# A seven-product feed-forward: four plain pairs first instead of two, the activations' sums on VectorE, and later products added in PSUM to copies that ScalarE writes there

## The chip, the cores and the metric

The kernel runs on one core of one Trainium2 chip. The metric is the device time of one execution in microseconds, and the time of a kernel is the median of its runs. The names of the engines in the rows are PE for TensorE, DVE for VectorE, ACT for ScalarE, POOL for GpSimd and SP for SyncE.

## The reference

Two layers of a hybrid backbone run over 640 tokens, 128 context tokens and 512 latent ones, with 1024 features. Each layer is a modulated norm, an input projection, four parallel mixers, a gated merge with an output projection, and then a second modulated norm with a SwiGLU feed-forward, which is what the change touches:

```python
def _swiglu(h, w1, w2):
    a = jnp.dot(h, w1)                     # (tokens, 1024) x (1024, 2 * 2816)
    gt, up = jnp.split(a, 2, axis=-1)
    return jnp.dot(jax.nn.silu(gt) * up, w2)

sh1, sc1, gt1, sh2, sc2, gt2 = _adaln(cvec, w_mod[l], b_mod[l])
x = x + gt1 * _merge(...)
x = x + gt2 * _swiglu(_modulate(_rmsnorm(x, norm2_g[l]), sh2, sc2), w_ffn_in[l], w_ffn_out[l])
```

All of it is float32. The shift, scale and gate rows come from an adaLN product of a condition vector with w_mod, twelve chunks of 512 columns a layer.

## The kernel before

Every float32 product is made of three fp32r matmuls: each operand is split into a rounded part (hi, a cast on ScalarE) and a remainder (lo, a subtraction on VectorE), and hi x hi, hi x lo and lo x hi are summed in PSUM. `split` (L450 to L453, rows L451 and L452) does this for activations and feed-forward halves, and `wload` (rows L402 and L403) for whole weight blocks. The matmuls of most of the kernel are issued by `mm3` (L414 to L416).

The activations of a layer lie transposed in `hT`: eight blocks of 128 features, two parts, 640 tokens. The feed-forward has 22 pairs of 128 gate columns and 128 up columns. They are worked in four groups of 6, 6, 6 and 4 pairs (`FF_SPLIT`), and after each group its 128-row pieces are multiplied with the down projection (`residual_tm`, or `norm_tm` after the last).

The first `FF_PLAIN` = 2 pairs of a layer are plain: gate and up are each computed for the tokens in two column groups of 256 and 384, with 8 x 3 matmuls for each, and the results go through `silu` (L1900) and `cb` (L1903). The other 20 pairs are seven-product pairs, a form of Winograd's variant of Strassen's multiplication. The two halves of the features and the two halves of the tokens (320 each) give A11, A12, A21 and A22. The feature halves of the gate's and the up's columns give B11, B21 (gate) and B12, B22 (up). The four results are the gate and the up of either half of the tokens, and they need seven products of half blocks instead of eight, each of 4 x 3 matmuls with 320 columns.

`ff_sums` (L1728) makes the sums of activations S1, S2, S3 and S4, one of four feature blocks at a time: two additions hi + lo of 128x640 (L1735), four sums and differences of 128x320 (L1740 to L1743) and three splits. S1 takes the place of A21 in `hT`, split once the last plain pair has read it (the splits at the end of the plain pairs in `layer`). `ff_sums` is a generator: `layer` runs two of its four steps after each of the two plain pairs, and all steps are done after the second.

`ff_load` (L1759) loads four half blocks of weights for a pair into a ring of six half buffers and makes the four differences t1 to t4 on GpSimd (L1770 to L1773). It then splits the seven operands in the order in which the products use them, through the rings `hi_ring` and `lo_ring` of five.

`ff_pair` (L1790) issues the seven products and what combines them. Three accumulators come from the ring `acc` of three banks and one from `bO`. VectorE adds the products out of PSUM into SBUF tiles (L1817, L1821, L1824, L1831, L1837), ScalarE copies the first product (L1814) and applies SiLU (L1828, L1832), and `out` (L1807) multiplies (L1809) and splits.

Between all this runs background work: `adaln_all` accumulates the adaLN chunks of this layer and of the next (L473, L475, L477 and L479, on ScalarE, GpSimd and VectorE), transposes the sums (`adaln_cols`, L481) and reduces them. `tick` takes a step of it at a rate of 0.2 for each step of the projections.

The program is written in one order. A planner that simulates the engines (`schedule_with_timeline_sim`) then lays down the order on each engine, by readiness and by the priorities that the code gives (`WPRI` for weights, `EPRI` for evictions). That order is fixed when the kernel runs.

Of the kernel before, what the change touches and what calls it, by code (L numbers as in the profile page):

```python
# [13 lines left out]
AF = mybir.ActivationFunctionType  # L14
ALU = mybir.AluOpType
AX = mybir.AxisListType

P = 128
# [59 lines left out]

FF_SPLIT = (6, 6, 6, 4)

FF_PLAIN = 2
HALF = 320

WPRI = 20000
EPRI = 500
# [139 lines left out]
def trunk(ctx: ExitStack, tc: tile.TileContext, a: dict, depth: int):  # L225
    nc = tc.nc
    V, S, G, T, SY = nc.vector, nc.scalar, nc.gpsimd, nc.tensor, nc.sync
# [116 lines left out]
    acc = ring("acc", 3, [P, 512], F32, pq)  # L344
    bS = ring("S", 2, [P, 512], F32, pq)
    bT = ring("T", 2, [P, 512], F32, pq)
    bO = ring("O", 1, [P, 512], F32, pq)
    bigs = Slots("big", 1, 5120)

    def r32(t, n=1280):  # L350
        return t[:, :n]
# [23 lines left out]
    hT = cp.tile([P, KT, 2, NTOK], F32R, name="hT")  # L375
# [31 lines left out]
    def run(gen):  # L407
        for _ in gen:
            tick()
# [40 lines left out]
    def split(hi, lo, src):  # L450
        i = S.copy(hi, src)  # L451
        V.tensor_tensor(lo, src, hi.bitcast(F32), ALU.subtract)  # L452
        return i  # L453
# [27 lines left out]
    def adaln_cols(dst, accs):  # L481

        for v in range(2):
            ps = (bT if v else bS)()
            for j in range(4):
                T.transpose(ps[:, j * P:(j + 1) * P], accs[v][:, P * j:P * j + P], ident)
            V.tensor_reduce(dst(v), ps.rearrange("p (j n) -> p j n", j=4), AX.X, ALU.add)
# [1240 lines left out]
    def ff_sums(held, s1):  # L1728

        sop = [[r32(held[2 * i + x]).rearrange("p (k w n) -> p k w n", k=2, w=2) for x in range(2)] for i in range(3)]  # L1730
        for k in range(4):
            x = [p640().rearrange("p (h n) -> p h n", h=2) for _ in range(2)]
            for i, c0 in enumerate((0, HALF)):
                hi, lo = [hT[:, k:k + 5:4, w, c0:c0 + HALF].bitcast(F32) for w in range(2)]
                (V if i and k % 2 == 0 else G).tensor_tensor(x[i], hi, lo, ALU.add)  # L1735
            (a11, a12), (a21, a22) = [(t[:, 0, :], t[:, 1, :]) for t in x]
            z = p640()
            s2, s3 = z[:, :HALF], z[:, HALF:]
            t1 = s1[:, HALF * k:HALF * k + HALF]
            V.tensor_tensor(t1, a21, a22, ALU.add)  # L1740
            V.tensor_tensor(s2, t1, a11, ALU.subtract)
            V.tensor_tensor(s3, a11, a21, ALU.subtract)
            V.tensor_tensor(a12, a12, s2, ALU.subtract)  # L1743
            for i, t in enumerate((s2, s3, a12)):
                o = sop[i][k // 2][:, k % 2]
                split(o[:, 0], o[:, 1], t)
            yield
# [11 lines left out]
    def ff_load(l, j, spare, ts):  # L1759

        parts = ff_halves(spare)
        with tc.high_priority(offset=WPRI):
            def half(tile, h):
                off, x = PLAN[("fi", tile)]
                t = parts()
                SY.dma_start(t, a["wflat"][l, off:off + P * x].rearrange("(p x) -> p x", p=P)[:, 512 * h:512 * h + 512])
                return t
            b11, b12, b22, b21 = half(2 * j, 0), half(2 * j + 1, 0), half(2 * j + 1, 1), half(2 * j, 1)
            t1, t2, t3, t4 = [t[:, :512] for t in ts]
            G.tensor_tensor(t1, b12, b11, ALU.subtract)  # L1770
            G.tensor_tensor(t2, b22, t1, ALU.subtract)
            G.tensor_tensor(t3, b22, b12, ALU.subtract)
            G.tensor_tensor(t4, b21, t2, ALU.subtract)  # L1773
        for x in (b11, t2, t3, t1, b21, t4, b22):
            with tc.high_priority(offset=WPRI):
                hi, lo = hi_ring()[:, :512], lo_ring()[:, :512]
                split(hi, lo, x)
            yield hi, lo
# [10 lines left out]

    def ff_pair(ops, b, at):  # L1790

        pa, pb, pc, pd = [t[:, :HALF] for t in (acc(), acc(), acc(), bO())]
        x, y, z = f640(), f640(), f640()
        h1, h2 = slice(0, HALF), slice(HALF, NTOK)
        u2, u3 = z[:, h1], z[:, h2]

        def prod(ps, name, first):
            w = next(b)

            more = dict(skip_group_check=not first)  # L1800
            for k in range(4):
                f = lambda part: w[part][:, k * P:(k + 1) * P]
                T.matmul(ps, f(0), ops[name](k, 0), start=first and k == 0, stop=False, **more)  # L1803
                T.matmul(ps, f(0), ops[name](k, 1), start=False, stop=False, **more)  # L1804
                T.matmul(ps, f(1), ops[name](k, 0), start=False, stop=k == 3, **more)  # L1805

        def out(sl):  # L1807
            with tc.high_priority(offset=EPRI):
                V.tensor_tensor(x[:, sl], x[:, sl], y[:, sl], ALU.mult)  # L1809
                split(at[:, 0, sl], at[:, 1, sl], x[:, sl])  # L1810

        prod(pa, "A11", True)
        with tc.high_priority(offset=EPRI):
            S.copy(u3, pa)  # L1814
        prod(pb, "S2", True)
        with tc.high_priority(offset=EPRI):
            V.tensor_tensor(u2, pb, u3, ALU.add)  # L1817
        yield
        prod(pc, "S3", True)
        with tc.high_priority(offset=EPRI):  # L1820
            V.tensor_tensor(u3, pc, u2, ALU.add)  # L1821
        prod(pd, "S1", True)
        with tc.high_priority(offset=EPRI):
            V.tensor_tensor(y[:, h2], pd, u3, ALU.add)  # L1824
        yield
        prod(pa, "A12", False)
        with tc.high_priority(offset=EPRI):
            S.activation(x[:, h1], pa, AF.Silu)  # L1828
        prod(pc, "A22", False)
        with tc.high_priority(offset=EPRI):  # L1830
            V.tensor_tensor(x[:, h2], pc, u2, ALU.add)  # L1831
            S.activation(x[:, h2], x[:, h2], AF.Silu)  # L1832
        yield
        out(h2)
        prod(pd, "S4", False)
        with tc.high_priority(offset=EPRI):
            V.tensor_tensor(y[:, h1], pd, u2, ALU.add)  # L1837
        out(h1)
        yield

    def layer(l, *start):
        d = {"of": {}, "m": [], "mg": []}
# [31 lines left out]
        sums = ff_sums(held, s1)  # L1874
        for g, cnt in enumerate(FF_SPLIT):
# [4 lines left out]
            for jx in range(cnt):  # L1880
                j = j0 + jx
# [9 lines left out]
                sl = pl.take(F32R)  # L1891
                at = r32(sl).rearrange("p (w n) -> p w n", w=2)
# [14 lines left out]
                for groups in (LATE, EARLY) if j == 0 else (GROUPS,):  # L1907
# [2 lines left out]
                        hook()  # L1910
                        hook = None
                    run(fm(wu, KT, hmov, cb, groups))
                next(sums, None)
                next(sums, None)
                if j == FF_PLAIN - 1:
                    for _ in sums:
                        pass
                    for k in range(4):
                        split(hT[:, k, 0, HALF:], hT[:, k, 1, HALF:], s1[:, HALF * k:HALF * k + HALF])
                    qs.give(s1)  # L1920
            if g == 0:
                gts = gate_rows(l, 1)
            if g == 3:
# [119 lines left out]
```

## Time and profile before

| | us |
|---|---|
| median of 3 runs | 2818.46 |
| lowest and highest run | 2810.98, 2820.67 |
| the profiled execution | 2822.84 |
| its span, first to last instruction | 2821.0 |
| TensorE busy | 2701.9 |
| VectorE busy | 2175.1 |
| ScalarE busy | 1440.7 |
| GpSimd busy | 782.8 |
| mean granted clock of TensorE | 0.982 |

Busy time of TensorE is the time in which at least one matmul is in flight; successive matmuls overlap, so the rate at which they are done is read from their start times. A granted clock of 1.00 is 2.4 GHz and 0.5 is 1.2 GHz; a number between them is a mean over both. The feed-forward of the first layer lies at about 950 to 1430 us, that of the second at about 2360 to 2800 us.

### The profile page before, as it was taken

What the parts mean: (1) busy time and instruction counts of PE and PEld (TensorE: products, weight loads), DVE (VectorE), ACT (ScalarE), POOL (GpSimd) and SP (SyncE); (2) the same over time, 40 slices, a digit from 0 to 9 for tenths busy, and PEclk for the clock granted to TensorE, in tenths of its full rate; (3) what the DMA queues carried; (4) which work ended last, traced back from release to release, by engine and by line L of the source; (5) the groups of instructions that cost most, each with busy time, mean ns of one, the idle gap of its engine ahead of it and who ended that gap; (6) DMA issues with size and microseconds to landing.
All of it is one profiled execution on the core that took longest, in us unless ns stands there. A gap on an engine that the chain in (4) does not pass through costs nothing.

```text
span 2821.0 us, 51942 instructions
## 1 busy us (share of the span) xinstructions
PE 2701.9 (96%) x19466; PEld 2642.6 (94%) x19466; DVE 2175.1 (77%) x4800; ACT 1440.7 (51%) x3314; POOL 782.8 (28%) x678
## 2 busy tenths in 40 slices
PE   8999999999999879999999999999999999999998
PEld 4998999999999768999899999999999999899998
DVE  7767768888973897978677867778888847876967
ACT  6864446665653443434358654456666534433423
POOL 2001212120132564453430101212111334353433
PEclk9999999999999889999999999999999999999999
DMA  7224322121233233232232323222121331322222
GB/s 282 88 85 123 96 78 83 53 73 59 68 121 128 87 115 120 79 109 90 68 108 92 107 85 120 89 72 76 48 81 57 124 123 61 92 74 90 80 82 79
DMA packets 124734, 264.30 MB, mean 94 GB/s; under 512 B 14321, under 2 KB 40273, under 8 KB 124481
## 3 DMA queue, kind: packets, MB, share of 16 engines
q1 hardware_dynamic: 124480, 260.97, 29.1%
q8 instruction: 153, 2.51, 0.4%
q14 instruction: 101, 0.82, 0.1%
HBM read 252.73 MB, written 7.95 MB: 92 GB/s over the span
## 4 chain that ended last, share of the span: by engine, by line
PE 74%; DVE 14%; ACT 5%; issue 3%; DMA 2%; POOL 1%; SPq 0%; DVEq 0%; POOLq 0%; ACTq 0%
PE acc L414 16%; PE acc L415 16%; PE acc L416 16%; PE acc L1803 3%; PE acc L1805 3%; PE acc L1804 3%; PE O L1224 2%; PE T L1214 2%; DVE msum L479 2%; DVE wlo L403 2%; DVE wlo L452 1%; DMA raw<-wflat 1%; PE O L1803 1%; PE O L1804 1%; PE O L1805 1%
## 5 line engine op out<-in xcount | busy, mean ns | idle before, releaser
L414 PE MATMUL acc<-hT,whi 128*128 128x256 f32 (+1 forms) x2112 | 667.0, 318 | 28.1 <-DVE hT L669 10.5
L415 PE MATMUL acc<-hT,whi 128*128 128x256 f32 (+1 forms) x2112 | 666.1, 316 | 6.0 <-DVE hT L670 4.5
L416 PE MATMUL acc<-hT,wlo 128*128 128x256 f32 (+1 forms) x2112 | 662.7, 314 | 1.0 <-DVE wlo L403 1.0
L402 ACT CAST whi<-raw 128x512 fp32r<-128x512 f32 (+1 forms) x472 | 289.4, 619 | 436.6 <-PE acc L415 172.8
L403 DVE TENSOR_TENSOR wlo<-raw,whi 128x512 fp32r<-128x512 f32 (+1 forms) x472 | 358.2, 764 | 145.9 <-ACT whi L402 135.1
L414 PEld LDWEIGHTS acc<-hT,whi 128*128 128x128 f32 x2112 | 404.2, 192 | 35.1 <-DVE hT L669 11.4
L415 PEld LDWEIGHTS acc<-hT,whi 128*128 128x128 f32 x2112 | 405.3, 192 | 9.5 <-DVE hT L670 5.7
L416 PEld LDWEIGHTS acc<-hT,wlo 128*128 128x128 f32 x2112 | 404.6, 192 | 2.1 <-DVE wlo L403 1.1
L475 POOL TENSOR_TENSOR msum<-msum,mtmp 128x512 f32<-128x512 f32 x140 | 210.9, 1507 | 267.8 <-ACT msum L473 153.9
L1604 POOL TENSOR_TENSOR m<-m,f 128x256 f32<-128x256 f32 x96 | 100.1, 1046 | 523.5 <-DVE f L1602 346.8
L1632 POOL TENSOR_TENSOR big<-big,t 128x256 f32<-128x256 f32 x150 | 122.2, 823 | 304.0 <-DVE t L1631 296.5
L1631 DVE TENSOR_TENSOR t<-acc,P 128x256 f32<-128x256 f32 x200 | 83.1, 420 | 122.6 <-PE acc L416 94.9
L729 ACT CAST pth<-T 128x512 fp32r<-128x512 f32 (+1 forms) x232 | 118.1, 521 | 114.7 <-PE T L1214 56.2
L730 DVE TENSOR_TENSOR ptl<-T,pth 128x512 fp32r<-128x512 f32 (+1 forms) x232 | 137.4, 601 | 41.7 <-ACT pth L729 39.7
L451 ACT CAST whi<-of 128x512 fp32r<-128x512 f32 x160 | 98.8, 619 | 134.7 <-PE acc L1804 54.8
L1803 PE MATMUL acc<-hT,whi 128*128 128x320 f32 x480 | 152.1, 317 | 13.5 <-DVE f L1821 8.8
L414 PE MATMUL acc<-whi,m 128*128 128x256 f32 x560 | 158.2, 284 | 5.2 <-DVE t L1631 5.1
L414 PE MATMUL acc<-big,whi 128*128 128x256 f32 (+1 forms) x512 | 159.0, 311 | 0.9 <-ACT f L1596 0.9
L415 PE MATMUL acc<-big,whi 128*128 128x256 f32 (+1 forms) x512 | 159.0, 311 | 0.0
L416 PE MATMUL acc<-big,wlo 128*128 128x256 f32 (+1 forms) x512 | 158.7, 311 | 0.0
L415 PE MATMUL acc<-wlo,m 128*128 128x256 f32 x560 | 157.8, 282 | 0.2 <-DVE wlo L403 0.2
L416 PE MATMUL acc<-whi,m 128*128 128x256 f32 x560 | 157.2, 281 | 0.0
(465 smaller groups left out, 8189.5 us busy)
## 6 DMA issues: line engine op xcount, KB each, us to landing
raw<-wflat SPq DMA_DIRECT2D x228, 512.0 KB
wm<-w_mod SPq DMA_DIRECT2D x160, 256.0 KB
raw<-wflat SPq DMA_DIRECT2D x131, 256.0 KB
q<-wflat SPq DMA_DIRECT2D x53, 256.0 KB
kv<-nbias SPq DMA_DIRECT2D x16, 576.0 KB
kv<-mdr SPq DMA_DIRECT2D x16, 320.0 KB
big<-x_sample SPq DMA_DIRECT2D x8, 512.0 KB
P<-gt_d SPq DMA_DIRECT2D x32, 128.0 KB
```

Of the source, the lines that this page charges most:

```text
L402: S.copy(hi[:, :n], raw[:, s0:s0 + n])
L403: V.tensor_tensor(lo[:, :n], raw[:, s0:s0 + n], hi[:, :n].bitcast(F32), ALU.subtract)
L414: T.matmul(ps, lhs(k, 0), rhs(k, 0), start=(k == 0), stop=False)
L415: T.matmul(ps, lhs(k, 0), rhs(k, 1), start=False, stop=False)
L416: T.matmul(ps, lhs(k, 1), rhs(k, 0), start=False, stop=(k == kn - 1))
L475: G.tensor_tensor(accs[v][:, :512], accs[v][:, :512], tmp, ALU.add)
L729: S.copy(hi[:, :n], ps[:, :n])
L730: V.tensor_tensor(lo[:, :n], ps[:, :n], hi[:, :n].bitcast(F32), ALU.subtract)
L1632: (V if n == 3 else G).tensor_tensor(xs[tt][:, 256 * n:256 * n + 256], xs[tt][:, 256 * n:256 * n + 256], t[:, :256], ALU.add)
L1803: T.matmul(ps, f(0), ops[name](k, 0), start=first and k == 0, stop=False, **more)
L1804: T.matmul(ps, f(0), ops[name](k, 1), start=False, stop=False, **more)
L1805: T.matmul(ps, f(1), ops[name](k, 0), start=False, stop=k == 3, **more)
```

## The change

Four pairs of a layer are plain instead of two, and one step of `ff_sums` follows each of them. All eight hi + lo additions of `ff_sums` are on VectorE; before, six of the eight were on GpSimd. In a seven-product pair the products are issued in another order (A11, S3, S2, A12, S1, A22, S4), and two of VectorE's additions are replaced: ScalarE copies the first bank into a bank of the ring S, the product of S2 is added onto that copy in PSUM, ScalarE copies the sum into the second bank of S and into SBUF, and the product of S1 is added onto that. The last half's multiplication reads its bank directly. The weights are loaded and subtracted in the order that this needs. The banks of the ring S are written once by a matmul with `start=True` after the plain pairs (`ff_prime`), so that later matmuls without it add to what stands there, and `adaln_cols` no longer uses that ring.

```diff
-FF_PLAIN = 2
+FF_PLAIN = 4
...
     def adaln_cols(dst, accs):
         for v in range(2):
-            ps = (bT if v else bS)()
+            ps = bT()
...
             for i, c0 in enumerate((0, HALF)):
                 hi, lo = [hT[:, k:k + 5:4, w, c0:c0 + HALF].bitcast(F32) for w in range(2)]
-                (V if i and k % 2 == 0 else G).tensor_tensor(x[i], hi, lo, ALU.add)
+                V.tensor_tensor(x[i], hi, lo, ALU.add)
...
-            b11, b12, b22, b21 = half(2 * j, 0), half(2 * j + 1, 0), half(2 * j + 1, 1), half(2 * j, 1)
+            b12, b22, b11, b21 = half(2 * j + 1, 0), half(2 * j + 1, 1), half(2 * j, 0), half(2 * j, 1)
             t1, t2, t3, t4 = [t[:, :512] for t in ts]
+            G.tensor_tensor(t3, b22, b12, ALU.subtract)
             G.tensor_tensor(t1, b12, b11, ALU.subtract)
             G.tensor_tensor(t2, b22, t1, ALU.subtract)
-            G.tensor_tensor(t3, b22, b12, ALU.subtract)
             G.tensor_tensor(t4, b21, t2, ALU.subtract)
-        for x in (b11, t2, t3, t1, b21, t4, b22):
+        for x in (b11, t3, t2, b21, t1, t4, b22):
...
-        pa, pb, pc, pd = [t[:, :HALF] for t in (acc(), acc(), acc(), bO())]
+        pa, pb, pc, pd = [t[:, :HALF] for t in (acc(), bS(), acc(), bS())]
...
-        u2, u3 = z[:, h1], z[:, h2]
+        u2, p7 = z[:, h1], z[:, h2]
...
-        def out(sl):
-            with tc.high_priority(offset=EPRI):
-                V.tensor_tensor(x[:, sl], x[:, sl], y[:, sl], ALU.mult)
-                split(at[:, 0, sl], at[:, 1, sl], x[:, sl])
+        early = lambda: tc.high_priority(offset=EPRI)
         prod(pa, "A11", True)
-        with tc.high_priority(offset=EPRI):
-            S.copy(u3, pa)
-        prod(pb, "S2", True)
-        with tc.high_priority(offset=EPRI):
-            V.tensor_tensor(u2, pb, u3, ALU.add)
+        with early():
+            S.copy(pb, pa)
+        prod(pc, "S3", True)
+        with early():
+            S.copy(p7, pc)
         yield
-        prod(pc, "S3", True)
-        with tc.high_priority(offset=EPRI):
-            V.tensor_tensor(u3, pc, u2, ALU.add)
-        prod(pd, "S1", True)
-        with tc.high_priority(offset=EPRI):
-            V.tensor_tensor(y[:, h2], pd, u3, ALU.add)
+        prod(pb, "S2", False)
+        with early():
+            S.copy(pd, pb)
+            S.copy(u2, pb)
+        prod(pa, "A12", False)
+        with early():
+            S.activation(x[:, h1], pa, AF.Silu)
         yield
-        prod(pa, "A12", False)
-        with tc.high_priority(offset=EPRI):
-            S.activation(x[:, h1], pa, AF.Silu)
+        prod(pd, "S1", False)
+        with early():
+            V.tensor_tensor(y[:, h2], pd, p7, ALU.add)
         prod(pc, "A22", False)
-        with tc.high_priority(offset=EPRI):
+        with early():
             V.tensor_tensor(x[:, h2], pc, u2, ALU.add)
             S.activation(x[:, h2], x[:, h2], AF.Silu)
         yield
-        out(h2)
+        with early():
+            V.tensor_tensor(x[:, h2], x[:, h2], y[:, h2], ALU.mult)
+            split(at[:, 0, h2], at[:, 1, h2], x[:, h2])
         prod(pd, "S4", False)
-        with tc.high_priority(offset=EPRI):
-            V.tensor_tensor(y[:, h1], pd, u2, ALU.add)
-        out(h1)
+        with early():
+            V.tensor_tensor(x[:, h1], pd, x[:, h1], ALU.mult)
+            split(at[:, 0, h1], at[:, 1, h1], x[:, h1])
         yield
+
+    def ff_prime():
+
+        for _ in range(2):
+            T.matmul(bS()[:, :HALF], hT[:, 0, 0, :P], hT[:, 0, 0, :HALF], start=True, stop=True)
...
-                next(sums, None)
-                next(sums, None)
+                next(sums)
                 if j == FF_PLAIN - 1:
-                    for _ in sums:
-                        pass
                     for k in range(4):
                         split(hT[:, k, 0, HALF:], hT[:, k, 1, HALF:], s1[:, HALF * k:HALF * k + HALF])
                     qs.give(s1)
+                    ff_prime()
```

## Rows read from the trace of the kernel before

**Rows 1.** The page, part 1: busy us of each engine, share, instructions.

```profile
PE 2701.9 (96%) x19466; PEld 2642.6 (94%) x19466; DVE 2175.1 (77%) x4800; ACT 1440.7 (51%) x3314; POOL 782.8 (28%) x678
```

**Rows 2.** Windows: stretch, its us, busy us of PE, PEld, DVE, ACT, POOL; clock, DMA.

```profile
955.00:998.00 43.00, 34.86 (x208) 33.59 (x208) 41.73 (x55) 19.98 (x42) 30.77 (x20) 0.85 0.30 98
998.00:1083.00 85.00, 64.76 (x362) 59.88 (x360) 84.19 (x112) 39.82 (x77) 50.17 (x33) 0.86 0.39 122
1132.20:1205.80 73.60, 73.60 (x507) 73.60 (x507) 67.05 (x95) 35.44 (x70) 29.27 (x20) 1.00 0.27 81
1365.90:1419.90 54.00, 48.27 (x300) 46.63 (x299) 41.42 (x61) 23.10 (x46) 18.01 (x12) 0.94 0.24 76
2395.80:2453.00 57.20, 52.05 (x338) 50.14 (x337) 52.17 (x83) 28.48 (x59) 19.80 (x13) 0.97 0.32 94
2730.00:2783.20 53.20, 48.90 (x330) 47.80 (x329) 44.91 (x65) 24.55 (x49) 16.61 (x12) 1.00 0.29 95
```

**Rows 3.** Timeline of TensorE: start us, us, operation (single matmuls).

```profile
991.17 0.28 PE L414 MATMUL acc<-hT,whi 128*128 128x256 f32 x1
...
993.91 0.33 PE L414 MATMUL acc<-hT,whi 128*128 128x384 f32 x1
...
998.07 0.31 PE L1803 MATMUL acc<-hT,whi 128*128 128x320 f32 x1
...
1132.26 0.31 PE L1803 MATMUL acc<-hT,whi 128*128 128x320 f32 x1
...
1205.58 0.31 PE L1805 MATMUL O<-kv,wlo 128*128 128x320 f32 x1
```

**Rows 4.** Waits of TensorE, 955 to 1083: us, times, longest us.

```profile
PE acc L1803 <- ACT hT L451: 6.2, 1, 6.2
```

**Rows 5.** Groups of VectorE, 998 to 1083: busy us, mean ns, idle before.

```profile
L479 DVE SCALAR_TENSOR_TENSOR msum<-wm,csil,msum 128x512 f32<-128x512 f32 x19 | 20.7, 1088 | 0.0
L452 DVE TENSOR_TENSOR wlo<-of,whi 128x512 fp32r<-128x512 f32 x16 | 16.6, 1041 | 0.3 <-ACT whi L451 0.3
...
L1809 DVE TENSOR_TENSOR f<-f,f 128x320 f32<-128x320 f32 x6 | 5.1, 844 | 0.0
L452 DVE TENSOR_TENSOR m<-f,m 128x320 fp32r<-128x320 f32 (+2 forms) x6 | 4.6, 774 | 0.0
L452 DVE TENSOR_TENSOR wlo<-q,whi 128x512 fp32r<-128x512 f32 x4 | 4.3, 1084 | 0.0
...
L1821 DVE TENSOR_TENSOR f<-acc,f 128x320 f32<-128x320 f32 x4 | 1.9, 477 | 0.0
```

**Rows 6.** Timeline of VectorE, single instructions.

```profile
959.42 0.81 DVE L1735 TENSOR_TENSOR P<-hT 128x640 f32<-128x640 f32 x1
...
1023.18 0.68 DVE L452 TENSOR_TENSOR wlo<-of,whi 128x512 fp32r<-128x512 f32 x1
1023.78 0.74 DVE L479 SCALAR_TENSOR_TENSOR msum<-wm,csil,msum 128x512 f32<-128x512 f32 x1
```

**Rows 7.** Groups of GpSimd, 955 to 1083.

```profile
L1735 POOL TENSOR_TENSOR P<-hT 128x640 f32<-128x640 f32 x6 | 11.5, 1936 | 1.4 <-DVE kv L452 1.4
...
L1771 POOL TENSOR_TENSOR of<-raw,of 128x512 f32<-128x512 f32 x3 | 4.8, 1605 | 0.0
```

**Rows 8.** Two lines of VectorE: duration ns min/median/max over the span.

```profile
L1821 DVE TENSOR_TENSOR f<-acc,f x40: 475/478/492, 1029.8 to 2776.3; 128x320 f32<-128x320 f32 x40
...
L1809 DVE TENSOR_TENSOR f<-f,f x80: 477/486/1606, 1038.0 to 2784.2; 128x320 f32<-128x320 f32 x80
```

**Rows 9.** Waits of TensorE in the last group of the first layer.

```profile
PE acc L1803 <- DVE f L1821: 4.3, 2, 2.3
```

**Rows 10.** Timeline of TensorE and ScalarE at a pair's end, second group.

```profile
1157.04 0.31 PE L1803 MATMUL acc<-hT,whi 128*128 128x320 f32 x1
...
1160.05 0.46 ACT L451 CAST m<-f 128x320 fp32r<-128x320 f32 x1 [2.22 <-DVE f L1809]
...
1160.94 0.42 ACT L1814 COPY f<-acc 128x320 f32<-128x320 f32 x1
```

## The prediction

> **What bounds the kernel now.** I read the page's engine shares first: TensorE is busy for 2701.9 of 2821.0 us [rows 1]. A gain therefore lies where TensorE stands still or runs at the lower clock, and the second view, the busy times by stretch, shows where in the feed-forward [rows 2]. In the second group of the first layer (1132 to 1206 us) TensorE fills the stretch at the full clock, so nothing is to be had there but less work. In the first group of the first layer (955 to 1083) it is busy for 34.9 of 43 and 64.8 of 85 us, with a granted clock of 0.85 and 0.86, while VectorE is busy for 41.7 of 43 and 84.2 of 85: VectorE sets the pace. The last group of the first layer, and the first and last groups of the second, lose a few us each.
>
> The start times of matmuls give what TensorE needs without waits [rows 3]. The six seven-product pairs of the second group run from 1132.26 to 1205.58 us and one more matmul: 73.5 us, 12.25 a pair, and a twelfth of a seventh, 0.146 us, a matmul; one product (12 matmuls) takes 1.75 us. A plain pair is 24 matmuls of 256 columns (991.17 to 993.91, 2.74 us) and 24 of 384 (993.91 to 998.07, 4.16 us), twice: 13.8 us. The four seven-product pairs of the first group take 85 us where four times 12.25 is 49: 36 us are lost to waits and clock.
>
> The waits of that stretch say on what: the longest is on a split of the activations after the plain pairs, 6.2 us [rows 4], the others on VectorE too. VectorE's groups there [rows 5] show three kinds of work: the remainders of the weights (16, 7 and 4 at 1.04 to 1.08 us; the first and the last row stand here, 28.3 us in all), the adaLN accumulations of the next layer, planned early (L479, 20.7 us), and the activation sums. They are also longer than they need be. Two neighbouring rows show a remainder at 0.68 and an accumulation at 0.74 us when nothing stretches them [rows 6]; their means here are 1.05 and 1.09, and GpSimd is busy for 50.2 of these 85 us.
>
> **The change part by part.** The sums below are against the profiled execution: 2821.0 us of span, 2822.84 us in all, 4.4 us above the median of the runs, so the same difference is taken from 2818.46.
>
> *Two more plain pairs a layer.* TensorE alone: four pairs at 13.8 instead of 12.25 is +6.2 us. In the first layer this hides behind VectorE, and it stands inside the stage sums below.
>
> *First layer, first group: 128 us (955 to 1083), of which VectorE is busy 125.9.* I count VectorE's time. A seven-product pair costs it a quarter of 28.3 for remainders, four PSUM additions of 0.48 (L1817, L1821 and the two like them, 1.9), two products at 0.84 (1.7) and two remainders of results at 0.77 (1.5): 12.2 us. A plain pair costs four remainders of 1.05, two products of 0.48 and two result remainders of about 0.8: 6.8. Two pairs change kind: -10.8. In the two that stay, VectorE loses two PSUM additions of 0.48 and one product of 0.84 (x times y for the first half now reads its bank directly): -3.6. The splits of S1's operand, which must wait for the last plain pair, now come before the fifth product instead of the fourth, with 7.0 us of cover instead of 5.3. The six sums that GpSimd did (11.5 us at 1.94 [rows 7]) come to VectorE at 0.81 each [rows 6], the same operation when it is alone: +4.9; were each as long as it is on GpSimd, +11.6. GpSimd loses these 11.5 us and eight weight subtractions of about 1.6: 24.4 us. VectorE's excess in the fast pairs, remainders 27 x 0.37, accumulations 19 x 0.35, products and sums about 4, is 21 us against 50.2 of GpSimd, 0.42 us for each, so up to -10; part of it is inside the -10.8, so I take -7, bounds 0 and -10. Together -16.5. Nothing better than TensorE's floor can come out: 43 as it is, two plain pairs (27.6) and two fast ones (24.5) are 95.1, so -32.9 is the far end; -2.8 is the near one (long sums, no relief). I take -16.5, since VectorE at 98% is what the rows show, and 111.5 us is still above the floor.
>
> The row says which additions are cheap to lose: those that read PSUM lie between 475 and 492 ns in all 40 cases, while the product of two SBUF tiles goes from 477 to 1606 [rows 8]. The Trainium skill, "SBUF — State Buffer", section "Who interferes with whom", says that a VectorE instruction with two SBUF inputs contends with a GpSimd instruction that reads SBUF, and one with at most one SBUF input does not. By this rule the change drops mostly additions that were never slowed, and each sum moved to VectorE takes two SBUF inputs: the stage would gain 9.5 rather than 16.5 (the relief of 7 gone) if GpSimd's adaLN additions keep hitting them. The trace agrees with the rule on which operations stretch.
>
> *Second layer, first group: 57.2 us against 49 [rows 2].* VectorE has no adaLN there. Floor after: 27.6 and 24.5, 52.1. I let a quarter of the 8.2 us loss stay: -3; ends -5.1 (none stays) and +3.1 (all of it).
>
> *Last groups: 54.0 and 53.2 us against 49 [rows 2].* In the first of them TensorE waits most for L1821, 4.3 us [rows 9]; that addition goes. I take -5 of 9.2, ends -9.2 and +4.
>
> *Products added to copies.* Here a wait is added. S2 may start only when ScalarE has copied the first accumulator into the second bank, and S1 only when it has copied S2's bank. Each has one product in between as cover, 1.75 us, for a copy of 0.42 us (the nearest row is L1814, from PSUM to SBUF [rows 10]; no row here writes PSUM from ScalarE, so 0.3 to 0.6). What stands ahead of the copy in ScalarE's queue are 0.62 us casts of weights and the casts of the results, which wait for VectorE. VectorE now needs one short product out of PSUM there in place of an addition, a stretched product and what lay between, so the casts come earlier than now. ScalarE has room: 35.4 of 73.6 us, plus three copies a pair of 0.42, 6 x 1.3, is 43. S4 also waits for the addition out of its bank with one product of cover instead of two. I take 0.1 us a pair over 36 pairs, +3.6; ends 0 and, as the rival below shows, much more.
>
> *The rest.* Weight order: the second product now needs one subtraction on GpSimd instead of two, nothing on TensorE's path; the DMA that reuses the last half buffer starts later, with over seven products of cover. Four extra priming matmuls: +0.6. The adaLN transposes take one bank ring instead of two: 20 pairs of them, and where the second waits for the reduction of the first it waits for a pass over as many columns as the accumulation of 0.74 us [rows 6], so at most 15 us; it is background work with nothing due behind it, so 0.
>
> Sum: -16.5 - 3 - 5 + 3.6 + 0.6 = -20.3 us: 2802.5 for the profiled execution, **2798** for the median.
>
> **The rivals.**
>
> *A. All the waits go.* The stages reach TensorE's floor: -32.9 - 5.1 - 9.2 + 0.6 = -46.6, 2772. For it: twenty more us of plain work with little VectorE load, in which the sums can be made. Against it: the adaLN accumulations stay and VectorE's sum is above the floor.
>
> *B. VectorE stays the bound.* The order on every engine is planned ahead, and adaLN work fills whatever the plan leaves free; with the long sums the first stage gives 2.8, the second layer's nothing, the last groups 2, the copies cost 3.6: about -1, 2817. For it: the accumulations of L479 that crowd this stage belong to the next layer and need not be done here. Against it: GpSimd loses 24 of 81 us.
>
> *C. The copies come late (slower).* In the steady group the cast of a result waited for VectorE until 1160.05, a weight cast followed, and the copy started at 1160.94, 3.90 us after the first matmul of A11 at 1157.04 [rows 10]. Two products are 3.50 us; with 0.42 for the copy, S2 would start 0.82 us late. If only the first copy of each pair is so late, 36 x 0.82 = 29.5 in place of 3.6, +5.6 in all, 2824. If both are, 59 and +35, 2853. I put it at 2838. It decides from 30 late copies of 72; from 40 the kernel is slower. For it: that wait occurs once in each steady pair. Against it: the stretched product that it waited for (1.57 us, L1809) has no place in the new second-half chain before the cast. The Trainium skill, "PSUM — Partial Sum Buffer", section "Engine vs sequencer instructions", says that the queues of ScalarE, VectorE and GpSimd are strictly first in, first out; by it a ready copy cannot pass a waiting cast. The rows agree: ScalarE stood still for 2.22 us with the copy two places behind.
>
> **How the numbers follow.** Forecast 0.50 (2785 to 2810 by itself), A 0.20, B 0.16, C 0.14. A measurement of this kernel can tell about 0.3%, 8.5 us, from no change: faster is below 2810, slower above 2827. Faster: the forecast's 0.47, A, and 0.05 of B, 0.72. Same: 0.03, B's 0.09, C's 0.04, 0.16. Slower: 0.02 of B and 0.10 of C, 0.12. The range goes from A to the first half of C: 2772 to 2825.
>
> **What would show it.** In the first layer's first group: its length from the norm to the first down projection near 112 us, granted clock above 0.9, VectorE still over 0.9 busy. In the steady groups 12.2 to 12.4 us a pair, with S2's and S1's waits on ScalarE in total under 5 us. Wrong would be a steady pair over 13 us with TensorE waiting on the copies (C), a first group that stays near 125 us (B), or one below 100 (A).

## The result, and the profile of the changed kernel

The changed kernel takes 2768.00 us (median of 4 runs, 2766.59 to 2768.38) against 2818.14 (4 runs, 2810.98 to 2820.67): ratio 0.9825, 95% interval 0.9807 to 0.9843. It is 50 us faster where 20 were forecast, and below the range, whose lower end was 2772. Its profiled execution took 2766.59 us, with a span of 2764.8; that of the kernel before was 4.7 us slower than the median of its runs, so the two profiles lie 6 us further apart than the medians.

The page of the changed kernel, part 1, as in [rows 1]:

```profile
PE 2681.5 (97%) x19518; PEld 2627.9 (95%) x19518; DVE 2051.2 (74%) x4672; ACT 1471.8 (53%) x3406; POOL 743.7 (27%) x650
```

TensorE is busy for 20 us less and idle for 36 less; VectorE loses 124 us. Where the 56.2 us between the two profiled spans lie:

| stretch | before | changed | only four plain pairs |
|---|---|---|---|
| start to first plain matmul, layer 0 | 948.4 | 943.0 | 941.5 |
| layer 0, first group | 134.5 | 102.6 | 102.8 |
| layer 0, rest of its pairs and down projections | 342.6 | 338.2 | 332.6 |
| of it pairs of groups 2, 3, last | 73.5, 73.5, 59.5 | 83.3, 76.6, 51.2 | 73.5, 73.5, 50.5 |
| to the feed-forward of layer 1 | 934.3 | 933.0 | 935.0 |
| layer 1, first group | 93.3 | 88.1 | 88.6 |
| rest, with its last group | 367.9, 54.4 | 359.9, 51.2 | 363.8, 50.2 |

The first group counts here from its first plain matmul to the last matmul of its seven-product pairs, and the last group of layer 0 to its real end at 1425.5; the window of [rows 2] stopped 5.5 us short of it. Lengths of pairs run from the start of their first matmul to that of their last, plus 0.145 us. The third column is the first experiment below.

Windows of the changed kernel, columns as in [rows 2]: layer 0 by groups, then the first and the last group of layer 1:

```profile
943.00:1045.60 102.60, 91.24 (x615) 88.75 (x614) 88.60 (x142) 52.16 (x108) 38.17 (x27) 0.95 0.39 123
1087.60:1171.00 83.40, 79.98 (x547) 78.46 (x547) 79.61 (x100) 49.33 (x102) 49.85 (x31) 1.00 0.38 118
1216.00:1292.60 76.60, 76.60 (x533) 76.60 (x532) 52.03 (x80) 43.84 (x90) 30.02 (x19) 1.00 0.28 87
1332.60:1383.80 51.20, 51.20 (x357) 51.20 (x356) 39.85 (x58) 30.06 (x64) 18.69 (x12) 1.00 0.32 102
2316.70:2404.90 88.20, 86.57 (x608) 85.98 (x607) 63.00 (x119) 42.78 (x92) 15.54 (x12) 1.00 0.30 98
2677.40:2728.70 51.30, 51.30 (x358) 51.30 (x357) 38.73 (x58) 30.77 (x64) 18.58 (x12) 1.00 0.28 93
```

The same two stretches of the kernel before, first group of layer 0 and a steady group of layer 1 with its down projection:

```profile
948.40:1083.00 134.60, 103.11 (x577) 96.49 (x577) 132.52 (x178) 61.55 (x123) 85.31 (x55) 0.85 0.38 120
...
2495.90:2612.30 116.40, 116.12 (x867) 115.91 (x866) 88.78 (x134) 44.46 (x85) 47.56 (x39) 1.00 0.26 82
```

In the first group VectorE falls from 132.5 of 134.6 us to 88.6 of 102.6, and GpSimd from 85.3 to 38.2: neither is the bound any more, and the granted clock goes from 0.85 to 0.95. Against that stands the second group of layer 0, which has got longer: 83.3 instead of 73.5 us.

VectorE's groups say why in both. First the kernel before in its first group, then the changed kernel there and (last row) in its second group:

```profile
L479 DVE SCALAR_TENSOR_TENSOR msum<-wm,csil,msum 128x512 f32<-128x512 f32 x29 | 33.4, 1150 | 0.1
```

```profile
L479 DVE SCALAR_TENSOR_TENSOR msum<-wm,csil,msum 128x512 f32<-128x512 f32 x14 | 13.7, 976 | 0.0
...
L1735 DVE TENSOR_TENSOR P<-hT 128x640 f32<-128x640 f32 x8 | 7.4, 944 | 0.0
...
L479 DVE SCALAR_TENSOR_TENSOR msum<-wm,csil,msum 128x512 f32<-128x512 f32 x14 | 15.8, 1126 | 0.5 <-DMA wm<-w_mod 0.4
```

Fifteen of 29 adaLN accumulations left the first group, and 14 stand in the second, where the kernel before had none. No edit says where they go: the planner put them elsewhere when the pairs changed. Of the 9.8 us that the second group grew, 3 are 26 matmuls of the down projection mixed in, as in the steady groups below.

The copies that S2 and S1 are added onto (the seeds) are neither late nor dear. By the profile no matmul waited for one of them (L1810 and L1817) in any of the 36 pairs. The timeline of a steady pair of layer 1 (ScalarE and TensorE), and the row of the copy from bank to bank:

```profile
2457.62 0.42 ACT L1810 COPY S<-acc 128x320 f32<-128x320 f32 x1
2457.97 0.45 ACT L451 CAST m<-f 128x320 fp32r<-128x320 f32 x1
...
2458.71 0.31 PE L1803 MATMUL S<-kv,whi 128*128 128x320 f32 x1
...
2460.47 0.31 PE L1803 MATMUL S<-kv,whi 128*128 128x320 f32 x1
...
2462.84 0.42 ACT L1817 COPY S<-S 128x320 f32<-128x320 f32 x1
...
2466.00 0.31 PE L1803 MATMUL S<-hT,whi 128*128 128x320 f32 x1
```

```profile
L1817 ACT COPY S<-S x36: 410/419/424, 1023.5 to 2720.1; 128x320 f32<-128x320 f32 x36
```

The seed copy ends at 2458.04. The product at 2458.71 is S4 of the pair before, which the plan puts in between; S2 starts at 2460.47, 2.4 us after its seed. S1 starts 2.7 us after the second seed (2463.26). The group with its down projection takes what it took, 116.3 us against 116.4 (row above):

```profile
2444.70:2561.00 116.30, 116.02 (x866) 115.81 (x865) 72.90 (x116) 51.48 (x103) 49.63 (x39) 1.00 0.26 82
```

Its pairs alone take 76.5 instead of 73.4 because the plan mixes in matmuls of the down projection (a window of 76.6 us holds 533 matmuls, one of 73.6 held 507 [rows 2]); the gap behind them is 3 us shorter.

### The profile page after: what moved, and what is told of

Read it like the earlier page. It is cut to its first block, busy times and chain, and to the rows that moved or that the text cites. A ratio compares the mean times of both kernels' runs of the same rounds, so it can differ in the third digit from the quotient of the medians.

```text
span 2764.8 us, 51796 instructions
## 1 busy us (share of the span) xinstructions
PE 2681.5 (97%) x19518; PEld 2627.9 (95%) x19518; DVE 2051.2 (74%) x4672; ACT 1471.8 (53%) x3406; POOL 743.7 (27%) x650
## 4 chain that ended last, share of the span: by engine, by line
PE 77%; DVE 11%; ACT 5%; issue 3%; DMA 2%; POOL 2%; SPq 0%; DVEq 0%; POOLq 0%; ACTq 0%
PE acc L414 17%; PE acc L415 17%; PE acc L416 17%; PE acc L1803 3%; PE acc L1804 3%; PE acc L1805 3%; PE O L1224 2%; PE S L1803 2%; PE S L1804 2%; PE S L1805 2%; PE T L1214 2%; DVE msum L479 1%; DVE wlo L403 1%; POOL msum L475 1%; PE S L1181 1%
## 5 line engine op out<-in xcount | busy, mean ns | idle before, releaser
L414 PE MATMUL acc<-hT,whi 128*128 128x256 f32 (+1 forms) x2240 | 701.0, 315 | 20.6 <-DVE hT L669 6.8
L415 PE MATMUL acc<-hT,whi 128*128 128x256 f32 (+1 forms) x2240 | 698.1, 312 | 2.2 <-DVE hT L612 1.4
L416 PE MATMUL acc<-hT,wlo 128*128 128x256 f32 (+1 forms) x2240 | 697.5, 312 | 0.8 <-DVE wlo L403 0.8
L402 ACT CAST whi<-raw 128x512 fp32r<-128x512 f32 (+1 forms) x488 | 299.7, 619 | 424.7 <-PE acc L415 198.0
L403 DVE TENSOR_TENSOR wlo<-raw,whi 128x512 fp32r<-128x512 f32 (+1 forms) x488 | 369.7, 761 | 154.0 <-ACT whi L402 146.3
L414 PEld LDWEIGHTS acc<-hT,whi 128*128 128x128 f32 x2240 | 424.0, 190 | 27.0 <-DVE hT L669 7.6
L415 PEld LDWEIGHTS acc<-hT,whi 128*128 128x128 f32 x2240 | 424.5, 190 | 5.5 <-DVE hT L612 2.1
L416 PEld LDWEIGHTS acc<-hT,wlo 128*128 128x128 f32 x2240 | 424.0, 189 | 1.8 <-DVE wlo L403 1.2
L1632 POOL TENSOR_TENSOR big<-big,t 128x256 f32<-128x256 f32 x150 | 127.9, 861 | 250.0 <-DVE t L1631 244.3
L452 DVE TENSOR_TENSOR wlo<-of,whi 128x512 fp32r<-128x512 f32 x144 | 129.4, 900 | 37.5 <-ACT whi L451 35.4
L451 ACT CAST whi<-of 128x512 fp32r<-128x512 f32 x144 | 88.7, 620 | 126.6 <-PE acc L416 51.9
```

Source lines behind the costliest of these rows:

```text
L402: S.copy(hi[:, :n], raw[:, s0:s0 + n])
L403: V.tensor_tensor(lo[:, :n], raw[:, s0:s0 + n], hi[:, :n].bitcast(F32), ALU.subtract)
L414: T.matmul(ps, lhs(k, 0), rhs(k, 0), start=(k == 0), stop=False)
L415: T.matmul(ps, lhs(k, 0), rhs(k, 1), start=False, stop=False)
L416: T.matmul(ps, lhs(k, 1), rhs(k, 0), start=False, stop=(k == kn - 1))
L1632: (V if n == 3 else G).tensor_tensor(xs[tt][:, 256 * n:256 * n + 256], xs[tt][:, 256 * n:256 * n + 256], t[:, :256], ALU.add)
```

## The experiments

Each ratio is against the kernel before on the same chip, with its 95% interval.

### One part at a time

**Only the plain pairs** (p_plain4), the rest as before:

```diff
-FF_PLAIN = 2
+FF_PLAIN = 4
-                next(sums, None)
-                next(sums, None)
+                next(sums)
```

> Only the four plain pairs (one step of the sums after each), the rest as before. Theory 1 (the plan: where adaLN accumulations of the next layer are put decides the first group of the first layer, and the two more plain pairs let the plan spread them): 25 to 40 us faster than before, first group of the first layer under 112 us, L479 count in it well below 29. Theory 2 (my accounting: VectorE's work in the stage falls by the 10.8 us of two pairs, adaLN stays): 5 to 12 us faster, L479 still near 29. Rival 3 (it is the copies that release VectorE): no faster than 6 us, since TensorE has 6.2 us more to do.

**Only the sums on VectorE** (v_sums):

```diff
-                (V if i and k % 2 == 0 else G).tensor_tensor(x[i], hi, lo, ALU.add)
+                V.tensor_tensor(x[i], hi, lo, ALU.add)
```

> Only the activations' sums on VectorE, two plain pairs, old products. Theory 1 says that GpSimd is what stretches VectorE and that the plan changes with it: 0 to 15 us faster. Theory 2 (accounting): +4.9 for the moved sums and -5 of relief (11.5 us of GpSimd at 0.42): within 5 us of before. Rival 3: within 3 us.

**Only the new products** (c_copies): the changed kernel with two lines of before, `FF_PLAIN = 2` (two steps of the sums after each plain pair) and six of the hi + lo sums on GpSimd.

> Only the new product order with the copies, its weight order, the priming and the adaLN transposes on one ring; two plain pairs, sums split between VectorE and GpSimd as before. Theory 1: 10 to 15 us faster, mostly in the last groups and the first group of the second layer. Theory 2 (accounting: 1.8 us for each of four pairs in the first group, 5 us in the last groups): about 12 us faster. Rival 3 (the copies make the gain): 30 us or more faster.

**All but the new products** (no_copies): four plain pairs, the sums on VectorE and the adaLN transposes on one ring, with `ff_pair` and `ff_load` of before and no priming.

> Four plain pairs, sums on VectorE, transposes on one ring, but the old products and weight order. Theory 1: 30 us or more faster than before, within 15 us of the changed kernel. Theory 2: 10 to 15 us faster. Rival 3: under 10 us faster.

**All but the plain pairs** (no_plain4): the changed kernel with two plain pairs, two steps of the sums after each.

> The changed kernel with two plain pairs (two steps of the sums after each): sums on VectorE, copies and one ring for the transposes remain. Its plan puts some 17 adaLN accumulations between the fast pairs' operations. Crowding: within 10 us of before (2806 to 2822), fast pairs of the first group over 75 us. My accounting (the relief by the other parts): 15 us or more faster than before.

**Three plain pairs, else as before** (p_plain3): one step of the sums after each of the first two pairs, two after the third.

> The kernel before with three plain pairs, sums in steps of 1, 1 and 2. Its plan has no adaLN accumulation between the operations of seven-product pairs, as with four. Crowding: 35 to 55 us faster than before, within 5 us of four plain pairs (TensorE has 3.1 us less to do), fast pairs of the first group near 12.5 us each. Room: about half of the gain, 20 to 30 us, with fast pairs of the first group over 15 us each.

| kernel | us | ratio |
|---|---|---|
| p_plain4 | 2766.39 | 0.982 [0.98, 0.9839] |
| v_sums | 2814.77 | 0.9992 [0.9983, 1.0001] |
| c_copies | 2815.60 | 0.9997 [0.9988, 1.0007] |
| no_copies | 2773.41 | 0.9846 [0.983, 0.9861] |
| no_plain4 | 2806.31 | 0.9968 [0.9958, 0.9978] |
| p_plain3 | 2793.99 | 0.9926 [0.9911, 0.994] |

The constant alone does all of it; the third pair is worth some 21 us and the fourth 28. These two steps are not alike. In layer 0's first group the third pair takes off 29.5 us (134.5 to 105.0) and the fourth 2.2 more. The rest of the fourth pair's 28 us is 13 in the last groups (54.7 and 58.9 us in p_plain3, 50.5 and 50.2 in p_plain4; see the section on them) and 12 in the stretch to the feed-forward of layer 1 (947.5 against 935.1), where no line differs but the order on the engines does; why the planner lays that stretch out otherwise is open. The other two parts do nothing alone, 9 us together without the plain pairs, and nothing on top of them; no_copies is 7 us slower than p_plain4 and took 946.3 us for that same stretch. The theory that the gain comes from lighter VectorE work in each pair falls with that. In the kernel with the constant alone the windows of the first two groups of layer 0, and VectorE's accumulations in the first, are:

```profile
941.50:1044.30 102.80, 88.61 (x578) 86.97 (x579) 88.52 (x136) 47.48 (x98) 49.07 (x32) 0.93 0.36 114
1089.00:1162.60 73.60, 73.60 (x507) 73.53 (x506) 68.74 (x95) 35.84 (x71) 30.35 (x21) 1.00 0.29 88
```

```profile
L479 DVE SCALAR_TENSOR_TENSOR msum<-wm,csil,msum 128x512 f32<-128x512 f32 x10 | 12.7, 1270 | 0.1
```

Ten accumulations instead of 29, all beside the plain pairs; of the other 19, 12 went into the down projections and 7 behind the last group, and the second group is at TensorE's 73.5 us.

### Where the adaLN work stands

Two theories were open: that the plain pairs free TensorE by themselves, and that they only make the planner move adaLN. First the accumulations were held back, or left out.

**Held behind the work written before them** (before_held, after_held): the accumulations of layer 1's first four chunks can't be planned ahead of what VectorE and ScalarE were given before them, and are written from the first down projection on.

```diff
+                prev = [last(e.engine) for e in (V, S)]
                 adaln_acc(msum, wm_tiles[(KT * i + k) % 4], k, mtmp)
+                if l and ch < 4:
+                    ...  # each new instruction ordered after prev on its engine
...
+        if l == 0:
+            bg[0] = 0.0       # layer 0's feed-forward begins
...
+                bg[0] = HELD if l == 0 else bg[0]      # after the first group, HELD = 0.4
```

> The kernel before with two plain pairs; the only change is that the second layer's first four adaLN chunks are kept, on VectorE and ScalarE, behind the work emitted before them, and their steps are emitted after the first group instead of during it. Nothing is left out. Theory of crowding (22 adaLN accumulations that the plan puts between the operations of the four fast pairs made these take 85 us instead of 49): fast pairs of the first group under 62 us, 15 to 30 us faster in all, some of it given back in the later groups. Rival, room (the sums need the time of two more plain pairs, whatever adaLN does): fast pairs over 75 us, under 8 us faster.

> The changed kernel with the same hold on the second layer's adaLN chunks. Crowding: its first group has little left to lose, the second group (83 us) falls towards 77 and other groups take a little: 2758 to 2768 us. Room: as the changed kernel, 2764 to 2772.

**Mostly left out** (before_noada, after_noada):

```diff
-                adaln_acc(msum, wm_tiles[(KT * i + k) % 4], k, mtmp)
+                if k == 0 or l == 0 or ch > 3:
+                    adaln_acc(msum, wm_tiles[(KT * i + k) % 4], k, mtmp)
```

> The kernel before, leaving out seven of eight accumulations of the second layer's first four adaLN chunks (their modulation is therefore not computed in full; loads stay). Crowding: fast pairs of the first group near 55 us, 25 to 40 us faster in all. Room: fast pairs over 75 us, under 10 us faster.

> The changed kernel with the same accumulations left out. Crowding: most is already gone, 5 to 15 us faster than the changed kernel (2753 to 2763). Room: within 5 us of it.

Held: 2824.18 us, 1.0028 [1.0016, 1.0041], and 2776.36, 0.9864 [0.9849, 0.9879]. Left out: 2794.63 us, 0.9931 [0.9916, 0.9946], and 2757.37, 0.9799 [0.9785, 0.9814]. Holding before's work empties the first group, whose seven-product pairs go from 84.8 to 60.5 us, and fills the third:

```profile
984.70:1045.20 60.50, 53.84 (x337) 52.05 (x338) 53.56 (x85) 29.36 (x60) 21.32 (x15) 0.94 0.26 81
...
1219.40:1318.20 98.80, 83.02 (x528) 80.73 (x527) 95.84 (x128) 46.53 (x88) 54.95 (x37) 0.93 0.34 107
```

The third group takes 98.8 us instead of 73.5, VectorE busy for 95.8 of them. Sixteen accumulations stand there now, and seven in the second group, which takes 84.9 us. So an accumulation costs TensorE time in whichever seven-product pair it stands. Held like this both kernels are slower than with adaLN as planned, because the work was written into the pairs of the second and third group; 15 to 30 us of gain were expected of before_held. Leaving accumulations out fell short too: before_noada's seven-product pairs in the first group still take 76.3 us, where 55 were expected, and seven accumulations that the edit keeps stand among them. Hence the next form.

**Only in the down projections** (after_res, plain4_res, before_res, no_plain4_res): held as above, but written at 0.4 inside layer 0's three down projections and not at all in its pairs.

```diff
+                bg[0] = HELD if l == 0 else bg[0]
                 for n in range(4):
                     residual_tm(xs, fo(n), cnt, lhs, gts, n)
+                bg[0] = 0.0 if l == 0 else bg[0]
```

> The changed kernel with the second layer's first four adaLN chunks kept on VectorE and ScalarE behind the work emitted before them, and their steps emitted only during the three down projections of the first layer. Crowding (an accumulation costs TensorE time between the operations of seven-product pairs, and little during a down projection): second group of the first layer 76 to 78 us instead of 83, all 3 to 8 us faster than the changed kernel (2760 to 2765). Room, or a cost wherever it is: as the changed kernel or slower, 2766 to 2776.

> The same hold in the kernel before with four plain pairs alone, whose plan already has these accumulations in the down projections: no change, 2763 to 2770, by either theory; faster by more than 3 us would say that the adaLN steps among its plain pairs cost something too.

> The kernel before, two plain pairs, with the second layer's first four adaLN chunks held in the three down projections; nothing else is changed. Crowding alone: the fast pairs of the first group at 60 us as in the earlier hold, the other groups at 73 to 76, 25 to 35 us faster than before. Room alone: under 10 us faster, fast pairs over 75. Both (my present theory: some 24 us of the 36 lost are crowding, 12 are sums that come too late): 20 to 30 us faster than before, 15 to 25 slower than four plain pairs alone.

> The changed kernel with two plain pairs and the hold in the down projections. Crowding alone: within 6 us of the changed kernel with the hold (2757 to 2763). Both: 10 to 25 us slower than that (2767 to 2782). Room alone: 2795 or more.

| products, sums | plain pairs | adaLN as planned | only in down projections |
|---|---|---|---|
| old | 2 | 2818.1 | 2801.36, 0.9946 [0.9931, 0.9961] |
| old | 4 | 2766.39, 0.982 | 2765.80, 0.9829 [0.9813, 0.9846] |
| new | 2 | 2806.31, 0.9968 | 2781.66, 0.9877 [0.9863, 0.9892] |
| new | 4 | 2768.00, 0.9825 | 2757.38, 0.9799 [0.978, 0.9818] |

Both theories hold in part. In the right column, with adaLN placed alike, four plain pairs still gain 36 us with the old products and 24 with the new. Not all of that is TensorE freed by plain pairs: 17 and 15 us lie in the two first groups (101.7 to 93.3 and 94.8 to 85.9 us with the old products, 104.2 to 98.4 and 96.8 to 88.1 with the new), and 10 and 7 in the last groups, where the constant also shifts a buffer ring (next section). Along a row, by the ratios, placing adaLN is worth some 15 and 26 us with two plain pairs, nothing in the old kernel with four, and 7 in the changed kernel (11 by the medians). The nothing is a sum: the first group of plain4_res is 9.5 us shorter than that of p_plain4 (102.8 to 93.3), and the last group of layer 0 is 8.5 longer (50.5 to 59.0). The changed kernel with adaLN in the down projections (after_res) has runs (2755.74 to 2763.37) that lie below all of the changed kernel's; of the kernels that leave nothing out only after3_res_phase below is as fast. Its first two groups in layer 0:

```profile
943.00:1041.40 98.40, 90.29 (x608) 88.32 (x607) 70.84 (x129) 48.49 (x102) 28.31 (x22) 0.95 0.33 104
1082.20:1160.30 78.10, 77.07 (x532) 76.58 (x532) 57.09 (x85) 45.96 (x94) 35.57 (x23) 1.00 0.31 95
```

The second group is 5 us shorter than with adaLN as planned, VectorE at 57 of 78 us. With adaLN out of the pairs the new products and sums are worth 8 us (2765.8 to 2757.4); as planned they were worth nothing. The 8 us aren't in the first group, which is 5 us longer with them (93.3 to 98.4); 4 are in the last group of layer 0 (59.0 to 54.6) and 5 in the stretch between the layers.

### The last groups

The last groups fell by 8.3 and 3.2 us, and also in p_plain4, where L1821 stays. Where adaLN stood as planned, their time went with the place in the ring of six half buffers (`half_at` modulo 6) at which they start. With the old products they took 50 to 51 us at place 2, 54.4 to 54.7 at 0 and 58.9 to 59.5 at 4, and with the new ones 51.2, 52.2 and 57.4 to 57.6. A seven-product pair moves the place on by four and a plain pair not at all, so `FF_PLAIN` shifts it.

**The ring's place set alone** (before_phase; plain3_phase with three plain pairs and += 2):

```diff
                 j = j0 + jx
+                if g == 3 and jx == 0:
+                    half_at[0] += 4
```

> The kernel before; ahead of the last group of each layer's pairs the ring of six half buffers for weights is turned on by four, so that the last group meets it at the place at which it meets it with four plain pairs. The last groups took 59.5 and 54.4 us before, 59 or 54.5 in every kernel with two or three plain pairs, by the ring's place, and 50 to 51 with four. Theory of the ring's place: 50 to 52 us each, 8 to 14 us faster in all. Rival (VectorE's load or adaLN work is what slows the last group): no change, within 4 us.

> Three plain pairs alone, with the ring of half buffers turned on by two ahead of each last group (the place of four plain pairs). Ring's place: last groups 50 to 52 us instead of 54.7 and 58.9, 2778 to 2786 in all instead of 2794. Rival: 2790 to 2797.

**Three plain pairs in the best form** (after3_res, and after3_res_phase with += 2):

> The changed kernel with three plain pairs and the hold in the down projections. Crowding alone: 1 to 3 us faster than with four (2754 to 2757), since TensorE has 3.1 us less to do. Both: within 5 us of it either way. Room alone: 10 us or more slower.

> The changed kernel with three plain pairs, the adaLN chunks held in the down projections, and the ring turned on by two ahead of each last group. Ring's place: last groups 51 to 53 us instead of 56.4, 2755 to 2761 in all instead of 2766. Rival: 2763 to 2768.

before_phase: 2808.95 us, 0.9977 [0.9967, 0.9986]; its last groups went from 59.5 to 50.1 and from 54.4 to 51.1, but the first group of layer 1, which the edit also starts at another place, from 93.3 to 97.4. plain3_phase: 2785.63, 0.9892 [0.9877, 0.9907], last groups 50.7 and 50.0 where p_plain3 had 54.7 and 58.9. after3_res: 2766.09, 0.9824 [0.9808, 0.9841]; after3_res_phase: 2758.90, 0.9798 [0.9783, 0.9813]: its last group in layer 1 went from 56.4 to 51.5, that of layer 0 stayed (56.4 and 56.7), a miss. What the place changes is who waits for a buffer. Window of layer 0's last group and the longest wait of SyncE's queue there (us, times, longest), first the kernel before, then before_phase:

```profile
1365.90:1425.50 59.60, 53.87 (x339) 52.23 (x338) 45.43 (x68) 25.77 (x51) 18.01 (x12) 0.94 0.27 85
```

```profile
SPq L397 <- DVE wlo L452: 30.6, 4, 16.3
```

```profile
1363.50:1413.60 50.10, 49.33 (x339) 49.04 (x338) 42.01 (x68) 25.32 (x51) 19.29 (x12) 1.00 0.30 95
```

```profile
SPq L397 <- DVE wlo L452: 16.0, 3, 10.5
```

The whole-block loads of L397 wait 30.6 us for a split that frees their buffer, and what is queued behind them is late; ScalarE's casts wait 12.2 us for weights from DMA in that stretch (5.3, 2.7, 2.4 and 1.8) and in the second none.

## Why the prediction was wrong

**The step that failed** is in the first group of layer 0: "I take -16.5, since VectorE at 98% is what the rows show, and 111.5 us is still above the floor." It gave 31.9 (134.5 to 102.6), beside the far end that the prediction took for TensorE's floor (-32.9). That was no floor, since it kept the first 43 us as they were: plain4_res does the stage in 93.3 us, 41.2 less. The sum counted what the edits take from VectorE and left all 29 adaLN accumulations standing. The changed plan has 14 there: 19.7 of the 43.9 us that VectorE lost in the stage are accumulations (33.4 to 13.7). Rival A named the case, and its objection, "the adaLN accumulations stay", was the false premise; rival B even said that this work "need not be done here" without drawing the sum from it. A's 2772 is 4 us from the result, in part by luck, since the last groups got there by another way (below). That adaLN is what filled the stage is shown by before_res: with two plain pairs and adaLN only in the down projections, the first group takes 101.7 us. It paid 12 us of that back in the rest of layer 0. A smaller slip of the same sum: it counts four PSUM additions of VectorE in a seven-product pair where there are five, 0.5 us a pair. Of the signs set down, the clock came (0.95) and VectorE's share did not (88.6 of 102.6 us); counted as in the prediction, from 6.6 us after the first plain matmul on, the group took 96 us, under the 100 that it named as the sign of A.

**The relief of 7 us** inside it isn't shown. v_sums takes the six sums from GpSimd and changes nothing that can be measured. On VectorE they took 0.81 us when alone and 0.94 in the mean (row L1735 above), near the end chosen (0.81). The Trainium skill, "SBUF — State Buffer", section "Who interferes with whom", gave 9.5 us for the stage in place of 16.5; the accumulations, two SBUF inputs each, went from 1.15 to 0.98 us in the mean as GpSimd's busy time there fell from 85 to 38 us, which agrees with the rule. The mean doesn't follow that busy time alone: in p_plain4 it is 1.27 us, with GpSimd busy for 49 of 102.8. Neither sum is what the stage did.

**Last groups, -5:** -11.5, for another reason, and beyond the far end of -9.2, which was read from windows that were too short: the groups took 59.5 and 54.4 us, 15.9 above 49 each. The prediction put them down to TensorE's wait for L1821 [rows 9]. Replacing that addition with two plain pairs left 57.4 and 52.2 us (c_copies), -2 each; setting the ring's place and nothing else gave 9.4 and 3.3. The wait on L1821 was where most of the lateness showed, not where it came from.

**Copies, +3.6:** 0 in the steady groups (232.7 us from the end of layer 1's first group to that of its third, in both kernels). A steady pair takes 12.75 us, above the 12.2 to 12.4 set down, but by the matmuls mixed in and not by a wait on the copies. Rival C is refuted. It held the cast ahead of the copy; the plan puts the copy first (2457.62, then 2457.97), and a product of the pair before in between. The Trainium skill, "PSUM — Partial Sum Buffer", section "Engine vs sequencer instructions", says that the queue is first in, first out. The rows of before agree (ScalarE idle for 2.22 us with the copy behind [rows 10]); in the pair shown here no copy stands behind a waiting cast, so it doesn't test the rule. What counted is the order laid down in the queue.

**First group of layer 1, -3:** -5.2 (93.3 to 88.1); the plain pairs alone give -4.7 (88.6), as the forecast had it. But with two plain pairs the new products made its four pairs longer, 57.3 to 66.7 us (c_copies) and 62.7 (no_plain4); why was not tried.

**Not of the change:** 5.4 us ahead of the first layer's feed-forward. p_plain4, v_sums, before_phase, before_res and before_noada run the kernel before's instructions there in the same order on TensorE, VectorE, ScalarE and GpSimd (up to 929 us), and reached the feed-forward at 941.5 to 948.2 us; the kernel before reached it at 948.4. So one execution differs from the next by as much. The remainder: layer 0 lost 3.9 us outside its first and last groups (longer pairs in the second and third group, with 14 accumulations in the second), layer 1 gained 4.8 behind its third group outside the last pairs, and 1.3 came between the layers. With -31.9, -11.5, -5.2 and -5.4 that is the -56.2 between the profiles.

**Open:** why the planner places adaLN otherwise at three and four plain pairs; why layer 0's last group takes 54.6 us in after_res and 59.0 in plain4_res at the good place. In both, SyncE's queue waits 5.1 us for buffers of adaLN loads in that group and the 3 us ahead of it, and not at all in the changed kernel or p_plain4; whether that is the cause was not tried.

## What to carry to other kernels

Where one planner orders all engines, an edit moves work that it does not touch: count the background work in each stage of the changed plan, or price the stage with it and without it, before taking a mean of the two. Work that is not due soon belongs where its engine has slack (here the down projections), and saying so to the planner was worth 7 to 26 us in three of four kernels. A loop count that changes how many ring buffers are used before a stage shifts the ring's place there; compare that before looking for a slow instruction.

## What the runs showed of the hardware

ScalarE copies a 128x320 tile from one PSUM bank to another in 0.42 us (410 to 424 ns in 36 cases), as long as from PSUM to SBUF (L1814, 0.42 [rows 10]). With the place of a buffer ring as the only edit, layer 0's last group took 50.1 us at a granted clock of 1.00 instead of 59.6 at 0.94 (before_phase and the kernel before).
